# Output projection by seven products: weight sums by accumulating loads, a block's tail taken in steps, SyncE's loads in one chain

## The chip, the core and the metric

The kernel runs on one core of a Trainium2 chip. The core has a TensorE (PE, with its weight loads shown apart as PEld), a VectorE (DVE), a ScalarE (ACT), a GpSimd (POOL) and a SyncE (SP), and 16 DMA engines that all of its DMA queues share. SP and POOL issue the DMAs here. The metric is the device time of one launch in microseconds (us), and what counts is the median of the runs.

## The reference

One transformer block on 512 tokens of width 2048, in float32. The change touches one step of it, the output projection with the residual:

```python
x = x + g_a[:, None, :] * (jnp.concatenate([y_conv, y_attn], axis=-1) @ w_out[l])
h = modulate(rms_norm(x, norm_ffn[l]), sh_f, sc_f)
x = x + g_f[:, None, :] * ((jax.nn.silu(h @ ffn_w1[l]) * (h @ ffn_w3[l])) @ ffn_w2[l])
```

Here `w_out` is 2048 x 2048, `y_conv` and `y_attn` are 512 x 1024 each, and `g_a` is a row of gates made from the conditioning vector. What comes ahead of it (norm, `w_in`, a short convolution, sparse attention) and behind it (the feed-forward part) is unchanged.

## The kernel before, in words

**Seven products.** The projection is a product of two matrices cut into 2 x 2 blocks, and the kernel computes it with seven block products in place of eight, numbered 1 to 7. For each it needs a sum of blocks of `y` (a "form") and a sum of blocks of `w_out`. A block of `w_out` is 1024 x 1024 and is handled in eight pieces j = 0 to 7 of 128 x 1024 (512 KB). The pieces of a product's weights are `WB[p, j]`. Products 1, 5, 6 and 4 share one buffer for each j, the tile `wt`, because their weights grow out of one another: first W11 alone (product 1), then plus W12 (product 5), then plus W22 (product 6), then plus W21 (product 4). Product 2 has W21 alone, product 3 has W22 alone, product 7 has W12 plus W22. Signs are in the forms.

**Units.** The work is a list `yu` of 56 units (p, j), in this order: products 2, 1 and 5 with their eight pieces each (units 0 to 23); then 6 and 3 interleaved (24 to 39); then 7 (40 to 47) and 4 (48 to 55). A unit is twelve matmuls of 128 x 128 by 512 (line 1242): four output tiles, and three matmuls for each, because every operand is split into a high and a low part of reduced precision. Products 1, 6, 7 and 4 accumulate in the PSUM banks called "x" (tag `aux`), 5 and 3 in "y" and 2 in "z" (tag `main`).

**What a unit needs.** `y_load` (line 1182) fetches the weights, `y_split` (line 1216) makes the high part on ACT (line 1231) and the low part on DVE (line 1233), and `y_form` (line 1038) does the same for the form (lines 1043 and 1044). The high and low parts go into rings of three places, so a split can be about two units ahead of the matmuls. Only the split of (7,7) has places of its own (the tiles `w77`), and those of (4,5) to (4,7) too (`w4`).

**Loads.** The buffers of products 2 and 3 and of some pieces of 7 come from a ring of four places of 512 KB (the tiles `raw`); (3,4), (3,5), (7,4) and (7,5) lie in a part of the large tile `x2T`, and (7,0), (7,1) in tiles of the form H6 once that form has been used. Plain loads are issued by SP (queue q1). Loads that add to what lies in the buffer (`added`, line 1178, DMA with an add) are issued by POOL (queue q0). For product 5 the kernel before does both: for j < 4, SP loads W12 into a `raw` place called "b", and DVE adds it to `wt` (`w_sum`, line 1438); for j of 4 and more, POOL adds it by the DMA itself. The sum for product 6, `wt` plus `WB[3, j]`, is always one of DVE's (line 1446); it needs (3, j) and must stand behind the split of (5, j), since it overwrites the same buffer.

**The residual.** The blocks of x are loaded too: block (1,1) and (1,2) into `x2T` (line 1332), (2,2) into tiles of the form H3 (line 1335), (2,1) later. When a block of the product is complete, DVE multiplies it with the gates (`ga`, loaded by POOL) and adds it to x; ACT takes the sum of squares for the norm; POOL stores it. For block (1,1) that is `first_block` (lines 1372 to 1377), for the fifth product's share of (2,2) `fifth`, for the sixth's share of (1,2) `sixth`.

**The order.** The loop at line 1485 goes through units 6 to 55. In step n it first takes what `steps_at[n]` holds (loads and sums, set with `at_unit`), then splits unit n + 2, then writes the matmuls of unit n, then takes what `behind[n]` holds (forms, tails, stores, set with `behind_unit`). The program is then turned into one queue of instructions for each engine when it is built. That step may set an instruction ahead of others that are written before it, when it takes it to be ready sooner; `tc.issue_after(i)` forbids that: what it encloses stands behind `i` in that engine's queue, without waiting for `i` to finish. At run time each engine takes its queue strictly in order.

Of the kernel before, what the change touches and what calls it, by code (L numbers as in the profile page):

```python
# [70 lines left out]
def block_kernel(ctx: ExitStack, tc: tile.TileContext, a: dict, out: bass.AP):  # L71
    nc = tc.nc
    w_in, ada_w, w_out = a["w_in"][0], a["ada_w"][0], a["w_out"][0]
    w1, w3, w2 = a["ffn_w1"][0], a["ffn_w3"][0], a["ffn_w2"][0]
    x = a["x"][0]
# [301 lines left out]
    for name, n in ROWS.items():  # L377
        src = a[name].rearrange("l (k p) -> (l k) p", p=P) if name != "conv_w" else \
# [453 lines left out]
    class EarlyPlaces:  # L832
        n = 0
# [217 lines left out]
    ybank = {}  # L1051
    WB = {}
# [57 lines left out]
    class Places:  # L1110
        n = 0
# [45 lines left out]
    def y_units():  # L1157
        yield from ((p, j) for p in (2, 1, 5) for j in range(HK))
        for j in range(0, HK, 2):
            yield from ((6, j), (6, j + 1), (3, j), (3, j + 1)) if j in (0, HK - 2) else ((6, j), (3, j), (6, j + 1), (3, j + 1))  # L1160
        yield from ((p, j) for p in (7, 4) for j in range(HK))

    yu = list(y_units())
    yat = {u: n for n, u in enumerate(yu)}

    def w_block(r, c, j):
        k = (r - 1) * HK + j
        return w_out[k * P:(k + 1) * P, (2 - c) * 1024:(3 - c) * 1024].rearrange("p (a b) -> p a b", a=4)

    def in_four(t):  # L1170
        return t.rearrange("p (a b) -> p a b", a=4)

    def ring_place():
        return in_four(ring[0].tile([P, 1024], F32, tag="raw", name="raw"))

    added_last, loaded_last = [], [None]

    def added(to, src):
        with tc.issue_after(added_last[-1]) if added_last else ExitStack():
            added_last.append(nc.gpsimd.dma_start(to, src, accum_op=ALU.add).ins)  # L1180

    def y_load(p, j):
        if p == 2:
            WB[p, j] = ring_place()
            nc.sync.dma_start(WB[p, j], w_block(2, 1, j))
        elif p == 1:
            for q in (1, 5, 6, 4):
                WB[q, j] = in_four(WT[j])
            nc.sync.dma_start(WB[p, j], w_block(1, 1, j))
        elif p == 5 and j < 4:  # L1190
            WB["b", j] = ring_place()
            nc.sync.dma_start(WB["b", j], w_block(1, 2, j))
        elif p == 5:
            added(WB[p, j], w_block(1, 2, j))
        elif p == 3:
            WB[p, j] = x2T[:, 4 * j - 8:4 * j - 4, 0:HS] if j in (4, 5) else ring_place()
            nc.sync.dma_start(WB[p, j], w_block(2, 2, j))
        elif p == 7:
            if j < 2:
                to = WB[p, j] = YF["H6"][2 * j:2 * j + 2]  # L1200
            else:
                WB[p, j] = x2T[:, 4 * j - 8:4 * j - 4, 0:HS] if j in (4, 5) else ring_place()
                to = [WB[p, j]]
            for c in (1, 2):
                for n, t in enumerate(to):
                    src = w_block(c, 2, j)[:, 4 // len(to) * n:4 // len(to) * (n + 1)]
                    if c == 1:
                        loaded_last[-1] = nc.sync.dma_start(t, src).ins
                    else:
                        added(t, src)  # L1210
        elif p == 4:
            added(WB[p, j], w_block(2, 1, j))
# [54 lines left out]
    for n in range(-5, 6):  # L1267
        if n + 5 < HK:
            y_load(*yu[n + 5])
        if n + 2 >= 0:  # L1270
            y_split(*yu[n + 2])
        if n >= 0:
            y_multiply(*yu[n])
# [34 lines left out]
    twos = {}  # L1308

    def x2_of(r, c, t, n):  # L1310
        if (r, c) == (1, 1):
            return x2T[:, 4 * t + 2 * n:4 * t + 2 * n + 2, HS:S]
        if (r, c) == (1, 2):
            return x2T[:, HK + 4 * t + 2 * n:HK + 4 * t + 2 * n + 2, HS:S]
        if (r, c) == (2, 2):
            return YF["H3"][2 * t + n]
        return in_four(twos["x", t])[:, 2 * n:2 * n + 2]

    def x_of(r, c, t):
        i = 2 * (r - 1) + t  # L1320
        return x[i * P:(i + 1) * P, (2 - c) * 1024:(3 - c) * 1024]

    def x_load(r, c):
        for t in range(2):
            if r == 2:
                twos["x", t] = t2p.tile([P, 1024], F32, tag="t2", name="x21")
                to = in_four(twos["x", t])
            else:
                k0 = (c - 1) * HK + 4 * t
                to = x2T[:, k0:k0 + 4, HS:S]  # L1330
            with tc.issue_after(loaded_last[-1]) if r == 2 else ExitStack():
                nc.sync.dma_start(to, x_of(r, c, t).rearrange("p (a b) -> p a b", a=4))

    def x22_load(t, n):
        nc.sync.dma_start(x2_of(2, 2, t, n), x_of(2, 2, t)[:, n * 512:(n + 1) * 512].rearrange("p (a b) -> p a b", a=2))
# [1 line left out]
    def x_store(r, c, t):  # L1337
        i = 2 * (r - 1) + t
        for n in range(2):
            to = xd[n][:, t, :] if (r, c) == (2, 2) else \  # L1340
                out[0, i * P:(i + 1) * P, (2 - c) * 1024 + n * 512:(2 - c) * 1024 + (n + 1) * 512]
            nc.gpsimd.dma_start(to.rearrange("p (a b) -> p a b", a=2), x2_of(r, c, t, n))

    tags = ["d1", "d2"] * 64

    def two():
        return dp.tile([P, 512], F32, tag=tags[-1], name=tags.pop()).rearrange("p (a b) -> p a b", a=2)

    def pair_of(ps):
        return ps.rearrange("p (a b) -> p a b", a=2)  # L1350

    def gate_of(c, n):
        return pair_of(ga[:, (2 - c) * 1024 + n * 512:(2 - c) * 1024 + (n + 1) * 512])

    def squared(r, c, t, n, junk):
        nc.scalar.activation(junk, x2_of(r, c, t, n), AF.Square,
                             accum_out=ss2[:, 2 * (r - 1) + t, 2 * (2 - c) + n:2 * (2 - c) + n + 1])
# [8 lines left out]
    def copies(bank):  # L1366
        for t in range(2):
            twos[bank, t] = t2p.tile([P, 1024], F32, tag="t2", name=f"c{bank}")
            for n in range(2):
                nc.scalar.copy(twos[bank, t][:, n * 512:(n + 1) * 512], ybank[bank][2 * t + n])  # L1370

    def first_block(t, n):
        u, x2 = two(), x2_of(1, 1, t, n)
        nc.vector.tensor_add(u, pair_of(ybank["x"][2 * t + n]), pair_of(twos["z", t][:, n * 512:(n + 1) * 512]))
        nc.vector.tensor_mul(u, u, gate_of(1, n))
        nc.vector.tensor_add(x2, x2, u)
        squared(1, 1, t, n, u)
# [56 lines left out]
    def at_unit(p, j, *todo):  # L1434
        steps_at.setdefault(yat[p, j], []).extend(todo)

    def w_sum(to, j, one):
        nc.vector.tensor_add(WB[to, j], WB[to, j], WB[one, j])

    for j in range(HK):  # L1440
        at_unit(*yu[6 + j // 4 if j < 7 else 9], (y_load, 1, j))
        at_unit(*yu[6 + j if j < 4 else 7 + j], (y_load, 5, j))
        if j < 4:
            at_unit(*yu[12 + j], (w_sum, 5, j, "b"))
        at_unit(*yu[(13, 14, 15, 16, 17, 19, 25, 26)[j]], (y_load, 3, j))
        at_unit(*yu[yat[6, j] - 4], (lambda j: nc.vector.tensor_add(WB[6, j], WB[6, j], WB[3, j]), j))
        at_unit(*yu[(24, 25, 28, 30, 32, 34, 37, 38)[j]], (y_load, 7, j))
        at_unit(*yu[(27, 31, 35, 39, 40, 41, 42, 43)[j]], (y_load, 4, j))
    for q in (2, 3, 0, 1):
        at_unit(2, 7, (lambda q: nc.gpsimd.dma_start(ga[:, q * 512:(q + 1) * 512], gad[q].to_broadcast([P, 512])), q))  # L1450
    at_unit(1, 2, (x_load, 1, 1))
    at_unit(1, 4, (x_load, 1, 2))
    for q in range(4):
        at_unit(*yu[24 + 2 * q], (x22_load, q // 2, q % 2))
    at_unit(7, 3, (x_load, 2, 1))
    behind = {}

    def behind_unit(p, j, *todo):
        behind.setdefault(yat[p, j], []).extend(todo)
# [3 lines left out]
            behind_unit(*yu[n], (y_form, p, j))  # L1463
    behind_unit(2, 7, (copies, "z"))
    for q, (t, n) in enumerate(TN):
        behind_unit(5, (0, 1, 3, 4)[q], (first_block, t, n))
        behind_unit(*yu[(30, 32, 33, 35)[q]], (fifth, t, n))
        behind_unit(7, q, (gated, 1, 2, t, n, "y"))
    for t in range(2):
        behind_unit(6, 0, (x_store, 1, 1, t))  # L1470
        behind_unit(4, 2, (x_store, 1, 2, t))
        behind_unit(4, 1, (x_store, 2, 2, t))
    behind_unit(5, 7, (copies, "y"))
    behind_unit(6, 7, (sixth,))
# [10 lines left out]
    for n in range(6, len(yu)):  # L1485
# [4 lines left out]
        p, j = yu[n]  # L1490
# [573 lines left out]
    q, held = -1, []  # L2064
    for n, (b, p, j) in enumerate(units):
# [18 lines left out]
        if n + 5 < len(units):  # L2084
            w_sum(*units[n + 5])
# [40 lines left out]
```

## Time and profile before

| What | us |
|---|---|
| median of 3 runs (lowest, highest) | 2147.44 (2147.4, 2149.01) |
| the profiled execution, its own time | 2148.66 |
| its span, first to last instruction | 2146.9 |
| PE busy | 2117.9 (99%) |
| DVE busy | 1773.1 (83%) |
| first and last start of the projection's matmuls (line 1242) | 673.35 and 846.5 |
| PE idle inside that stretch, in two gaps | 0.68 and 8.33 |

The page gives each engine's busy time over the span. A row of a queue in order of time gives start, length, engine, line, operation, what it writes and reads, and in brackets how long the engine was idle before it and what ended that. A row of a stretch gives its length and then the busy time of PE, PEld, DVE, ACT and POOL, each with its number of instructions, then the clock that was granted to PE, the DMA engines' share and GB/s. In the DMA view a queue's row has packets, MB and its share of the 16 engines' time.

### The profile page before, as it was taken

How to read it: one execution, taken by the hardware profiler on the slowest of the kernel's cores; microseconds unless marked ns; L12 is line 12 of the kernel's file. 1: busy time of each engine (PE TensorE's matmuls, PEld its weight loads, DVE VectorE, ACT ScalarE, POOL GpSimd, SP SyncE). 2: the span in 40 equal slices, each digit the busy share in tenths (PEclk: the TensorE clock that was granted, in tenths of full speed). 3: DMA queues.
4: the chain of work that ended last, by engine and by line, in shares of the span. 5: the costliest groups of instructions: out<-in, count | busy, mean ns of one | idle time of the engine just before them, and what ended most of it. 6: DMA issues, size and time to landing. Idle time of an engine off the chain costs nothing.

```text
span 2146.9 us, 30986 instructions
## 1 busy us (share of the span) xinstructions
PE 2117.9 (99%) x11453; PEld 1778.9 (83%) x11453; DVE 1773.1 (83%) x2596; ACT 1043.2 (49%) x1665; POOL 254.9 (12%) x326
## 2 busy tenths in 40 slices
PE   7999999999999989999999999999999999999999
PEld 6778778888888868888888888888888887888887
DVE  7788658888788977888888888888888887878788
ACT  5226244555555547644444444444444555444543
POOL 0000200000000220001111111111111122211110
PEclk9999999999999999999999999999999999999999
DMA  9985638756668984598878877888787599797975
GB/s 339 363 272 192 201 100 252 217 163 206 179 184 272 258 199 138 139 248 206 201 191 189 209 196 187 203 195 203 184 202 182 144 301 295 145 307 138 290 157 139
DMA packets 452234, 450.20 MB, mean 210 GB/s; under 512 B 20707, under 2 KB 379147, under 8 KB 451442
## 3 DMA queue, kind: packets, MB, share of 16 engines
q1 hardware_dynamic: 379678, 333.00, 50.2%
q0 software_dynamic: 71872, 114.74, 26.9%
q8 instruction: 90, 1.47, 0.3%
q10 hardware_dynamic: 532, 0.48, 0.1%
q14 instruction: 62, 0.51, 0.1%
HBM read 428.19 MB, written 19.96 MB: 209 GB/s over the span
## 4 chain that ended last, share of the span: by engine, by line
PE 89%; DVE 4%; DMA 4%; issue 1%; SPq 1%; ACT 1%; ACTq 0%; DVEq 0%; POOLq 0%
PE main L1582 15%; PE aux L1582 11%; PE aux L1981 9%; PE main L1981 9%; PE main L1588 8%; PE aux L1588 6%; PE main L121 5%; PE main L123 5%; PE main L122 5%; PE aux L1242 2%; PE aux L121 2%; PE aux L989 2%; PE aux L123 2%; PE aux L122 2%; DMA raw<-in_w_out 1%
## 5 line engine op out<-in xcount | busy, mean ns | idle before, releaser
L1569 ACT CAST whi<-raw 128x1024 fp32r<-128x1024 f32 x246 | 257.6, 1051 | 259.1 <-PE main L1582 122.1
L1582 PE MATMUL main<-hC,whi 128*128 128x512 f32 x1408 | 347.1, 392 | 0.3 <-ACT whi L1569 0.2
L1576 DVE TENSOR_TENSOR wlo<-raw,whi 128x1024 fp32r<-128x1024 f32 x218 | 266.1, 1221 | 86.1 <-PE aux L1588 42.0
L1569 ACT CAST whi<-t 128x1024 fp32r<-128x1024 f32 x186 | 195.5, 1051 | 248.1 <-PE main L1981 62.1
L1582 PEld LDWEIGHTS main<-hC,whi 128*128 128x128 f32 x1408 | 256.9, 188 | 53.1 <-DVE d L1601 2.7
L1582 PE MATMUL aux<-hC,whi 128*128 128x512 f32 x1072 | 264.4, 391 | 0.0
L1582 PEld LDWEIGHTS aux<-hC,whi 128*128 128x128 f32 x1072 | 196.3, 188 | 38.2 <-issue 0.6
L1588 PEld LDWEIGHTS main<-hC,wlo 128*128 128x128 f32 x1408 | 184.9, 191 | 7.8
L1588 PE MATMUL main<-hC,wlo 128*128 128x256 f32 x1408 | 191.2, 283 | 0.0
L121 PE MATMUL main<-alo,whi 128*128 128x512 f32 x432 | 174.2, 404 | 0.0
L123 PE MATMUL main<-ahi,whi 128*128 128x512 f32 x432 | 170.3, 395 | 0.0
L122 PE MATMUL main<-ahi,wlo 128*128 128x512 f32 x432 | 169.1, 391 | 0.0
L1588 PE MATMUL aux<-hC,wlo 128*128 128x256 f32 x1072 | 148.5, 282 | 0.0
L1953 DVE TENSOR_TENSOR wlo<-t,whi 128x1024 fp32r<-128x1024 f32 x102 | 124.2, 1220 | 29.1 <-ACT whi L1569 29.0
L1588 PEld LDWEIGHTS aux<-hC,wlo 128*128 128x128 f32 x1072 | 142.1, 191 | 6.4
L1576 DVE TENSOR_TENSOR wlo<-t,whi 128x1024 fp32r<-128x1024 f32 x84 | 102.6, 1221 | 37.3 <-issue 13.4
L1981 PE MATMUL main<-wlo,ghi 128*128 128x512 f32 x304 | 118.5, 390 | 1.4 <-DVE wlo L1953 1.2
L1981 PE MATMUL aux<-whi,glo 128*128 128x512 f32 x308 | 119.8, 389 | 0.0
L1981 PE MATMUL aux<-whi,ghi 128*128 128x512 f32 x308 | 119.8, 389 | 0.0
L1981 PE MATMUL aux<-wlo,ghi 128*128 128x512 f32 x308 | 119.7, 389 | 0.0
L1981 PE MATMUL main<-whi,ghi 128*128 128x512 f32 x304 | 118.3, 389 | 0.0
L1981 PE MATMUL main<-whi,glo 128*128 128x512 f32 x304 | 118.3, 389 | 0.0
(426 smaller groups left out, 4173.7 us busy)
## 6 DMA issues: line engine op xcount, KB each, us to landing
raw<-in_ffn_w SPq DMA_DIRECT2D x204, 512.0 KB, 5.7
t<-in_ffn_w POOLq DMA_DIRECT2D x90, 512.0 KB, 6.8
t<-in_ffn_w SPq DMA_DIRECT2D x78, 512.0 KB, 5.9
araw<-in_ada_w SPq DMA_DIRECT2D x56, 512.0 KB, 8.7
raw<-in_w_in SPq DMA_DIRECT2D x128, 192.0 KB, 4.0
raw<-in_w_in SPq DMA_DIRECT2D x38, 512.0 KB, 4.9
kT<-in_ada_w SPq DMA_DIRECT2D x35, 512.0 KB, 4.4
accs<-in_ada_w POOLq DMA_DIRECT2D x64, 256.0 KB, 4.9
```

The source lines that it names most:

```text
L121: nc.tensor.matmul(ps, lhs[0], rhs[1], start=first, stop=False)
L122: nc.tensor.matmul(ps, lhs[1], rhs[0], start=False, stop=False)
L123: return nc.tensor.matmul(ps, lhs[0], rhs[0], start=False, stop=last).ins
L989: nc.tensor.matmul(po[:, b * HD:(b + 1) * HD], s["pT"][b][:, kb * P:(kb + 1) * P], vv[b][:, kb, g * HD:(g + 1) * HD], start=kb == 0, stop= ...
L1242: nc.tensor.matmul(ps, l, w, start=m == 0 and j == 0 and p in (1, 5, 2), stop=m == 2 and j == HK - 1 and p in (3, 2, 4), skip_group_check= ...
L1569: hi_ins[-1] = nc.scalar.copy(hi, t).ins
L1576: lo_ins[-1] = nc.vector.tensor_sub(lo, t, hi.bitcast(F32)).ins
L1582: nc.tensor.matmul(ps, wt[0][:, k * P:(k + 1) * P], hc(p, k), start=first and k == 0, stop=False, skip_group_check=True)
L1588: nc.tensor.matmul(ps[:, HS:], wt[1][:, k * P:(k + 1) * P], hc(p, k)[:, 0:HS], start=False, stop=last and k == HK - 1, skip_group_check=True)
L1953: W["last"] = nc.vector.tensor_sub(lo, t, hi.bitcast(F32)).ins
L1981: nc.tensor.matmul(ps[2 * t + c], x_[:, j, tok], w[:, cs], start=m == 0 and j == 0 and p in (1, 5, 2), stop=m == 2 and j == GS[b] - 1 and ...
```

## The change

There are five edits in the projection.

- The weight sums of product 5 are all made by accumulating loads on POOL: the four "b" loads of SP, their `raw` places and DVE's four sums are gone. The load for (5, j) stands at step 7 + j.
- A helper `chained` puts loads of SP into one chain, each behind the one before in SP's queue: x of blocks (1,1) and (1,2), (3,0) to (3,5) and the parts of (7,0) and (7,1) that SP loads. By the steps the chain runs x (1,1), x (1,2), (3,0) to (3,3), (7,0), (3,4), (7,1), (3,5). The loads of (3,4) and (3,5) go from steps 17 and 19 to 24 and 25, those of (3,0) to (3,3) from 13 to 16 to 15 to 18, x (1,1) one step forward.
- `first_block` is cut in two. `first_sum` (the add that empties the PSUM bank) stays behind the fifth product's units; the multiplication, the add to x and the squares go behind units 25, 27, 29 and 31. `fifth` goes from behind units 30, 32, 33, 35 to behind 33, 35, 38, 39.
- The stores of block (1,1) go from behind unit 24 to behind unit 33. Those of block (1,2) go from behind (4,2) to behind (7,1) and (7,3), and into the chain of POOL's accumulating loads.
- The accumulating loads (4,4) to (4,7) go from steps 40 to 43 to steps 42, 42, 44, 44.

```diff
-    added_last, loaded_last = [], [None]
+    added_last, loaded_last, chain = [], [None], []
+
+    def chained(to, src):
+        with tc.issue_after(chain[-1]) if chain else ExitStack():
+            chain.append(nc.sync.dma_start(to, src).ins)
+        return chain[-1]
...
-        elif p == 5 and j < 4:
-            WB["b", j] = ring_place()
-            nc.sync.dma_start(WB["b", j], w_block(1, 2, j))
         elif p == 5:
             added(WB[p, j], w_block(1, 2, j))
         elif p == 3:
             WB[p, j] = x2T[:, 4 * j - 8:4 * j - 4, 0:HS] if j in (4, 5) else ring_place()
-            nc.sync.dma_start(WB[p, j], w_block(2, 2, j))
+            (chained if j < 6 else nc.sync.dma_start)(WB[p, j], w_block(2, 2, j))
...
-                        loaded_last[-1] = nc.sync.dma_start(t, src).ins
+                        loaded_last[-1] = chained(t, src) if j < 2 else nc.sync.dma_start(t, src).ins
...
-            with tc.issue_after(loaded_last[-1]) if r == 2 else ExitStack():
-                nc.sync.dma_start(to, x_of(r, c, t).rearrange("p (a b) -> p a b", a=4))
+            src = x_of(r, c, t).rearrange("p (a b) -> p a b", a=4)
+            if r == 1:
+                chained(to, src)
+                continue
+            with tc.issue_after(loaded_last[-1]):
+                nc.sync.dma_start(to, src)
...
-            nc.gpsimd.dma_start(to.rearrange("p (a b) -> p a b", a=2), x2_of(r, c, t, n))
+            with tc.issue_after(added_last[-1]) if (r, c) == (1, 2) else ExitStack():
+                stored = nc.gpsimd.dma_start(to.rearrange("p (a b) -> p a b", a=2), x2_of(r, c, t, n)).ins
+            if (r, c) == (1, 2):
+                added_last.append(stored)
...
+    block1 = {}
+
+    def first_sum(t, n):
+        u = block1[t, n] = two()
+        nc.vector.tensor_add(u, pair_of(ybank["x"][2 * t + n]), pair_of(twos["z", t][:, n * 512:(n + 1) * 512]))
+
     def first_block(t, n):
-        u, x2 = two(), x2_of(1, 1, t, n)
-        nc.vector.tensor_add(u, pair_of(ybank["x"][2 * t + n]), pair_of(twos["z", t][:, n * 512:(n + 1) * 512]))
+        u, x2 = block1[t, n], x2_of(1, 1, t, n)
...
-        at_unit(*yu[6 + j if j < 4 else 7 + j], (y_load, 5, j))
-        if j < 4:
-            at_unit(*yu[12 + j], (w_sum, 5, j, "b"))
-        at_unit(*yu[(13, 14, 15, 16, 17, 19, 25, 26)[j]], (y_load, 3, j))
+        at_unit(*yu[7 + j], (y_load, 5, j))
+        at_unit(*yu[(15, 16, 17, 18, 24, 25, 25, 26)[j]], (y_load, 3, j))
...
-        at_unit(*yu[(27, 31, 35, 39, 40, 41, 42, 43)[j]], (y_load, 4, j))
+        at_unit(*yu[(27, 31, 35, 39, 42, 42, 44, 44)[j]], (y_load, 4, j))
...
-    at_unit(1, 2, (x_load, 1, 1))
+    at_unit(1, 1, (x_load, 1, 1))
...
-        behind_unit(5, (0, 1, 3, 4)[q], (first_block, t, n))
-        behind_unit(*yu[(30, 32, 33, 35)[q]], (fifth, t, n))
+        behind_unit(5, (0, 1, 3, 4)[q], (first_sum, t, n))
+        behind_unit(*yu[(25, 27, 29, 31)[q]], (first_block, t, n))
+        behind_unit(*yu[(33, 35, 38, 39)[q]], (fifth, t, n))
         behind_unit(7, q, (gated, 1, 2, t, n, "y"))
     for t in range(2):
-        behind_unit(6, 0, (x_store, 1, 1, t))
-        behind_unit(4, 2, (x_store, 1, 2, t))
+        behind_unit(*yu[33], (x_store, 1, 1, t))
+        behind_unit(7, (1, 3)[t], (x_store, 1, 2, t))
```

More of the change, by code (lines that the diff above doesn't have):

```diff
@@ L1435, in at_unit @@
         steps_at.setdefault(yat[p, j], []).extend(todo)
-    def w_sum(to, j, one):
-        nc.vector.tensor_add(WB[to, j], WB[to, j], WB[one, j])
     for j in range(HK):
         at_unit(*yu[6 + j // 4 if j < 7 else 9], (y_load, 1, j))
-        at_unit(*yu[6 + j if j < 4 else 7 + j], (y_load, 5, j))
-        if j < 4:
-            at_unit(*yu[12 + j], (w_sum, 5, j, "b"))
-        at_unit(*yu[(13, 14, 15, 16, 17, 19, 25, 26)[j]], (y_load, 3, j))
+        at_unit(*yu[7 + j], (y_load, 5, j))
+        at_unit(*yu[(15, 16, 17, 18, 24, 25, 25, 26)[j]], (y_load, 3, j))
         at_unit(*yu[yat[6, j] - 4], (lambda j: nc.vector.tensor_add(WB[6, j], WB[6, j], WB[3, j]), j))
         at_unit(*yu[(24, 25, 28, 30, 32, 34, 37, 38)[j]], (y_load, 7, j))
-        at_unit(*yu[(27, 31, 35, 39, 40, 41, 42, 43)[j]], (y_load, 4, j))
+        at_unit(*yu[(27, 31, 35, 39, 42, 42, 44, 44)[j]], (y_load, 4, j))
     for q in (2, 3, 0, 1):
         at_unit(2, 7, (lambda q: nc.gpsimd.dma_start(ga[:, q * 512:(q + 1) * 512], gad[q].to_broadcast([P, 512])), q))
-    at_unit(1, 2, (x_load, 1, 1))
+    at_unit(1, 1, (x_load, 1, 1))
     at_unit(1, 4, (x_load, 1, 2))
```

## The prediction, made before the result was known

> **What bounds the kernel now.** I read the page first, then the stretches of the output projection, then the queues of TensorE (PE), VectorE (DVE), ScalarE (ACT), SyncE (SP) and GpSimd (POOL) there in order of time, and last the DMA queues in short windows.
>
> ```profile
> span 2146.9 us, 30986 instructions
> PE 2117.9 (99%) x11453; PEld 1778.9 (83%) x11453; DVE 1773.1 (83%) x2596; ACT 1043.2 (49%) x1665; POOL 254.9 (12%) x326
> ```
>
> PE is idle for 29 us of 2146.9; every other engine can only cost time through those gaps. The change touches the projection alone (673 to 849 us), so what it can win is the idle time there, and what it can lose is a new gap.
>
> ```profile
> 753.80 0.50 PE L1242 MATMUL main<-wlo,form 128*128 128x512 f32 x1 [0.68 <-DVE wlo L1233]
> 753.80 3.06 PE main L1242 x12
> 756.85 2.72 PE aux L1242 x12
> 800.54 0.80 PE L1242 MATMUL aux<-wlo,form 128*128 128x512 f32 x1 [8.33 <-DVE wlo L1233]
> 801.13 1.05 PE L1242 MATMUL aux<-whi,form 128*128 128x512 f32 x2
> 804.56 0.61 PE L1242 MATMUL aux<-whi,form 128*128 128x512 f32 x2
> ```
>
> There are two gaps. A unit is 12 matmuls and takes 2.72 us (second chain row). After the first gap (0.68 us) a unit took 3.06, so that gap costs 0.68 + 0.34 = 1.0 us. After the second (8.33 us) the ten matmuls from 800.54 to 804.56 took 4.02 us where the pace is 10 x 2.72/12 = 2.27, so it costs 8.33 + 1.75 = 10.1 us. The doubled spacing is a clock matter: pairs take 1.05 and then 0.61 us. [...]
>
> What holds each gap? The second one first:
>
> ```profile
> 783.89 0.84 POOL L1180 DMA_DIRECT2D raw<-in_w_out  x1 [1.11 <-DVE wlo L1233]
> 797.15 1.14 ACT L1231 CAST w<-raw 128x512 fp32r<-128x512 f32 x2 [11.70 <-DMA raw<-in_w_out]
> 798.19 1.04 ACT L1231 CAST whi<-raw 128x1024 fp32r<-128x1024 f32 x1
> ```
>
> The two 512-wide casts are the split of (7,7), the only one in halves of a place of its own (w77). In ACT's queue it stands ahead of the split of (7,3), which PE needs four units earlier, and it waits for its accumulating load, issued at 783.89 and landed at 797.15. So an engine's queue does not follow the written order: it was laid down as if loads landed sooner than they do. DVE shows the same habit:
>
> ```profile
> 715.05 1.22 DVE L1233 TENSOR_TENSOR wlo<-wt,whi 128x1024 fp32r<-128x1024 f32 x1
> 716.52 1.22 DVE L1446 TENSOR_TENSOR wt<-wt,raw 128x1024 f32<-128x1024 f32 x1
> 717.66 1.21 DVE L1233 TENSOR_TENSOR wlo<-wt,whi 128x1024 fp32r<-128x1024 f32 x1
> 720.32 0.39 PE L1242 MATMUL main<-wlo,form 128*128 128x512 f32 x1
> ```
>
> Row 716.52 is the first L1446, the sum that adds the third product's weights (3,0) to place 0. It is written at step 20, beside the splits of units 21 and 22, yet it stands right behind the low part of (5,0) (715.05) and ahead of that of (5,1) (717.66), which PE uses at 720.32, at the start of unit 17. It did not wait, since (3,0) had landed. This place decides my forecast.
>
> **The change, part by part.** *Removed: four loads "b" and four sums.*
>
> ```profile
> L1192 SPq DMA_DIRECT2D raw<-in_w_out x4: 328/328/328, 682.5 to 690.2; - x4
> L1438 DVE TENSOR_TENSOR wt<-wt,raw x4: 1215/1216/1217, 698.3 to 706.1; 128x1024 f32<-128x1024 f32 x4
> ```
>
> 4 x 1.22 = 4.9 us of DVE go between 698 and 707. No PE gap lies there, and the low part of (5,1) was done at 718.87, 1.45 us ahead of its use: worth 0.
>
> *Added: four accumulating loads for (5,0) to (5,3).* Each can start when the low part of (1,j) is written, which for (1,0) is at 694.05 + 1.22 = 695.3, ten microseconds ahead of the first one now:
>
> ```profile
> 694.05 1.22 DVE L1233 TENSOR_TENSOR wlo<-wt,whi 128x1024 fp32r<-128x1024 f32 x1
> L1180 POOL DMA_DIRECT2D wt<-in_w_out x4: 840/858/895, 706.4 to 713.5; - x4
> DMA to landing us min/median/max: 8.3/10.1/11.3
> ```
>
> POOL's four issues (0.86 us each) hide, as it is 12% busy. For their own splits they land in time: (5,0) by 695.3 + 11.3 = 707, nine microseconds before its unit starts at 720.32 - 2.72 = 717.6, the others in turn. What matters is whom they meet. Windows 711:722 (accumulating loads running), 705:710 (almost none) and 701:706 (the gate loads `ga`) of the DMA view, then 694:700:
>
> ```profile
> q0 software_dynamic: 492, 1.82, 82.8%
> q1 hardware_dynamic: 488, 0.81, 22.8%
> ...
> q1 hardware_dynamic: 970, 1.72, 90.0%
> q0 software_dynamic: 47, 0.13, 11.0%
> ...
> q0 software_dynamic: 270, 0.88, 61.4%
> q1 hardware_dynamic: 487, 0.52, 32.2%
> ...
> q1 hardware_dynamic: 1158, 1.42, 74.5%
> q0 software_dynamic: 2, 0.01, 0.5%
> ```
>
> q0 is POOL's queue, q1 is SP's. Beside accumulating loads the two go packet for packet (492 to 488), and q1 gets 488/11 = 44 packets per us; alone it gets 970/5 = 194. The accumulating packets take nearly all the time, so whatever SP loads then crawls. [...]
>
> *Moved: SP's chain x, x, (3,0) to (3,3), (7,0), (3,4), (7,1), (3,5).*
>
> ```profile
> 694.21 0.93 SPq L1332 DMA_DIRECT2D x2T<-in_x  x2
> 696.29 0.99 SPq L1332 DMA_DIRECT2D x2T<-in_x  x2
> 699.51 5.54 SPq L1197 DMA_DIRECT2D raw<-in_w_out  x3
> ```
>
> SP's four loads of x write rows of 256 numbers, 1 KB packets: 4 x 512, and with (1,7) between them 128 more of 4 KB, 2176 in all. (3,0) is issued behind them, at about 697.3 instead of 699.5, since its ring place no longer waits for a "b". At 700, 1158 of the 2176 had gone (last pair of rows), and 1018 remain. Now the count: (5,0) with its 128 packets (512 KB at 4 KB) takes 128 of the 1018 along (2.9 us at 44 per us); `ga`, 256 packets, takes 256 x 487/270 = 460 (about 5 us); 430 are left at about 708. Before, q0 then rests until the accumulating load of 706.4 starts; now (5,1) to (5,7) follow without a pause (seven times about 3 us), so 430 packets of x at 44 per us last until 717.5, and the 128 packets of (3,0), 4 KB now and thus slower, until about 721.5. [...]
>
> With the sum (6,0) at its old place in DVE's queue, queued behind it are the low part of (5,1), the first sums and all later low parts. DVE waits until 724, sums (1.14), writes the low part (1.21), and PE starts unit 17 at 726.4 instead of 720.3: a new gap of 6.1 us, with a slow start of 1.75 (nearer to the gap of 8.33 than to that of 0.68). Bounds: 0 at a landing of 717.9, 11 + 1.75 at 729. (3,1) lands some 3 us later, by when DVE has work in hand: 0.
>
> *(3,4) and (3,5) behind (7,0), (7,1).*
>
> ```profile
> 735.59 1.01 SPq L1208 DMA_DIRECT2D H<-in_w_out  x1
> 744.12 1.21 DVE L1446 TENSOR_TENSOR wt<-wt,x2T 128x1024 f32<-128x1024 f32 x1
> ```
>
> The first row is the last load of (7,1), the second the sum that needs (3,5). If (3,5) follows that load at 736.6 and lands as slowly as the load of 743.55 further down (waited for until 751.38, 7.8 us), it is there at 744.4: 0, at most 3 if DVE, no longer behind, gets there sooner.
>
> *The first block in two parts, the fifth's later.* Eight operations (0.68 us, 0.60 apart, 4.8 us) leave DVE's full stretch for steps 25 to 31, and eight like them leave steps 30 to 35 for 33 to 39.
>
> ```profile
> 715.00:730.00 15.00, 15.00 (x68) 12.43 (x67) 15.00 (x21) 9.18 (x15) 0.56 (x1) 1.00 0.88 244
> 745.00:760.00 15.00, 14.32 (x63) 11.50 (x62) 13.10 (x19) 7.17 (x11) 0.84 (x1) 1.00 0.62 168
> 760.00:775.00 15.00, 15.00 (x68) 12.43 (x67) 11.56 (x16) 7.75 (x12) 3.02 (x3) 1.00 0.86 193
> 742.32 1.21 DVE L1233 TENSOR_TENSOR wlo<-raw,whi 128x1024 fp32r<-128x1024 f32 x1
> 743.55 0.33 SPq L1197 DMA_DIRECT2D raw<-in_w_out  x1
> 751.38 1.23 DVE L1446 TENSOR_TENSOR wt<-wt,raw 128x1024 f32<-128x1024 f32 x1 [1.90 <-DMA raw<-in_w_out]
> ```
>
> DVE (fifth column, after PE and PEld) has 1.9 and 3.4 us free in the later stretches, room for what comes net; without it up to 3 us would show. The relief also explains the only gain: the first gap hangs on (3,6), loaded at 743.55 when the low part of (3,0) is out of the ring place (743.53), and DVE waits for it at 751.38. A DVE that isn't behind writes that part about 1.2 us sooner, more than the 0.68: the gap goes, -1.0.
>
> *x's stores.* Those of block (1,1) (0.54 us each on POOL at their best) move to step 33, where POOL is 0.84 of 15 busy: 0. Those of (1,2) now stand between the accumulating loads (4,3) and (4,4) and wait for DVE's sums of that block, which sit behind the second gap (its end is 800.54). So (4,4) to (4,7), issued ahead of that gap now, are issued after it, some 15 us later. They stand behind (7,7) either way, so its landing is the same. They belong to the projection's last four units: with 10.1 us to land (the row of POOL's loads above) they come in time, taken as 0, at most 4 if a split of theirs stands early in ACT's queue.
>
> **Sum**, against the profiled execution (2148.66, a span of 2146.9 and 1.8 around it): 2148.66 + 6.1 + 1.75 - 1.0 = 2155.5. That execution lies 1.2 above the median of 2147.44, so the median comes to **2154.3 us**, slower by 0.3%.
>
> **Rivals.** *Loads in time.* If (3,0) lands by 717.9, or the sum stands later in DVE's queue, only the first gap goes: 2147.44 - 1.0 = 2146.4. For it: "b" is gone from SP's queue, and alone that queue moves 194 packets per us, by which the 1018 + 128 packets would take 5.9 us from 700 on and (3,0) would be there by about 708.5. Against it: the 44 packets per us. [...]
>
> *The second gap closes (faster).* If the split of (7,7) gets behind that of (7,3) in ACT's queue, or its load lands 9 us sooner, the 10.1 us go with the first gap's 1.0: 2136.3, or about 2144 with the new gap beside it. For it: queue orders are laid down anew with each edit. Against it: the loads that lead to (7,7) keep their steps, and the stores that now wait in the chain come behind it.
>
> *The store chain (slower).* The splits of (4,5) to (4,7) have places of their own as (7,7) has, and if they stand early in ACT's queue ACT waits for loads issued some 15 us later. Once ACT waits longer than the 2.72 us of a unit, PE stands: +2 to +4, 2150.5 without the new gap, 2158 with it.
>
> **How the numbers follow.** A change under 0.2% (4.3 us) can't be told from none. New gap at (6,0): 0.55, of which 0.41 come out over 4.3 us and 0.14 under. Loads in time: 0.20, no difference. Second gap closes: 0.18, faster. New gap and second gap closed: 0.03, no difference. Store chain alone: 0.04, half of it over 4.3. That makes faster 0.18, same 0.39, slower 0.43. The range leaves out the far end of the second gap's closing and the worst landing: 2139 to 2163; the forecast's own range is 2147 to 2163.
>
> **What would show it.** Right: a PE gap at about 720 released by DVE's wlo; an L1446 sum waiting for a w_out DMA just ahead of it; x2T loads taking over 20 us to land; the gap at 753 gone, that at 792 still there. Wrong: no wait at the first L1446 (the packet count failed), or a queue order in which that sum stands later, or (7,7)'s casts behind (7,3)'s.

## The result, and the profile after

The changed kernel takes **2159.49 us** (median of 4 runs, 2158.29 to 2163.08), the kernel before 2148.23 in the same comparison: ratio 1.0055, 95% interval 1.0038 to 1.0073, **11.3 us slower**. The forecast was 6.9 us slower (2154.3, range 2139 to 2163). The profiled execution took 2158.29.

The top of its page, then PE's longest waits over the whole kernel (sum, times, longest):

```profile
span 2156.5 us, 30990 instructions
PE 2119.5 (98%) x11453; PEld 1780.6 (83%) x11453; DVE 1768.7 (82%) x2592; ACT 1042.6 (48%) x1665; POOL 258.0 (12%) x330
```
```profile
PE aux L1245 <- DVE wlo L1236: 9.3, 1, 9.3
PE main L1245 <- DVE wlo L1236: 9.1, 1, 9.1
```

DVE does 4.4 us less (the four sums), and PE waits 9 us more. The 8.33 us wait of before is still there as the first row; the second is new. In the changed kernel `y_mm` is line 1245 (1242 before), the casts are 1234 (1231), the low parts 1236 (1233), the sums for product 6 1456 (1446), the accumulating loads 1186 (1180).

The new wait, in DVE's queue, ACT's and PE's in order of time, then the stretch 730:732 (its clock is the third number from the end):

```profile
713.65 1.23 DVE L1236 TENSOR_TENSOR wlo<-wt,whi 128x1024 fp32r<-128x1024 f32 x1 [1.16 <-ACT whi L1234]
714.79 0.42 DVE L1044 TENSOR_TENSOR form<-H,form 128x256 fp32r<-128x256 f32 x1
726.81 1.23 DVE L1456 TENSOR_TENSOR wt<-wt,raw 128x1024 f32<-128x1024 f32 x1 [11.60 <-DMA raw<-in_w_out]
727.96 0.68 DVE L1386 TENSOR_TENSOR d<-aux,cz 128x512 f32<-128x512 f32 x1
728.56 1.21 DVE L1236 TENSOR_TENSOR wlo<-wt,whi 128x1024 fp32r<-128x1024 f32 x1
```
```profile
715.28 1.05 ACT L1234 CAST whi<-wt 128x1024 fp32r<-128x1024 f32 x1 [1.36 <-PE aux L1245]
```
```profile
729.83 0.79 PE L1245 MATMUL main<-wlo,form 128*128 128x512 f32 x1 [9.14 <-DVE wlo L1236]
730.42 1.05 PE L1245 MATMUL main<-whi,form 128*128 128x512 f32 x2
733.70 0.39 PE L1245 MATMUL main<-wlo,form 128*128 128x512 f32 x1
```
```profile
730.00:732.00 2.00, 2.00 (x5) 1.61 (x6) 2.00 (x3) 0.00 (x0) 0.00 (x0) 0.50 1.03 335
```

The sum (6,0) stands where it stood before, right behind the split of (5,0), but now (3,0) is not there: DVE is idle for 11.60 us. Behind it in the queue stands a step of the first block (727.96) and then the low part that PE needs for unit 17, (5,1)'s (728.56). That low part had nothing to wait for: its cast on ACT (715.28) was done 10 us earlier. PE waits 9.14 us, and then starts slowly: the nine matmuls from 729.83 to 733.70 take 3.87 us where the pace of before is 9 x 2.72/12 = 2.04, and the granted clock was 0.50 in 730:732. DVE took its queue in order here: it spent the 11.60 us in front of work that was ready.

Why (3,0) was late: SP's queue, then the DMA view of 705:727.

```profile
696.50 8.35 SPq L1180 DMA_DIRECT2D raw<-in_w_out  x4
```
```profile
q0 software_dynamic: 1042, 3.73, 80.8%
q1 hardware_dynamic: 1047, 1.80, 24.7%
wt<-in_w_out POOLq DMA_DIRECT2D x4, 512.0 KB, 19.7
```

(3,0) is the first of the four, issued at 696.50 and in use at 726.81, 30 us later. For 22 us the two queues go packet for packet (1042 to 1047), and POOL's packets take 81% of the engines' time: 0.808 x 16 x 22 / 1042 = 273 ns each on average, against 83 ns for one of SP's by the same working. SP's queue gets 48 packets per us. The four accumulating loads issued in this stretch took a median of 19.7 us to land.

The second gap, in POOL's, ACT's and PE's queues:

```profile
794.18 0.84 POOL L1186 DMA_DIRECT2D raw<-in_w_out  x1 [0.95 <-DVE wlo L1236]
808.64 1.14 ACT L1234 CAST w<-raw 128x512 fp32r<-128x512 f32 x2 [12.69 <-DMA raw<-in_w_out]
809.69 1.04 ACT L1234 CAST whi<-raw 128x1024 fp32r<-128x1024 f32 x1
812.04 0.79 PE L1245 MATMUL aux<-wlo,form 128*128 128x512 f32 x1 [9.32 <-DVE wlo L1236]
```

The casts of (7,7) still stand ahead of (7,3)'s, and wait 12.69 us for a load issued at 794.18; 9.32 us of PE against 8.33. The first gap of before is gone: DVE still waits for (3,6), but briefly, and PE not at all (SP's queue, then DVE's):

```profile
754.12 0.33 SPq L1200 DMA_DIRECT2D raw<-in_w_out  x1
```
```profile
758.83 1.22 DVE L1456 TENSOR_TENSOR wt<-wt,raw 128x1024 f32<-128x1024 f32 x1 [1.12 <-DMA raw<-in_w_out]
```

So the projection loses 9.1 + 1.8 for the new gap and 1.0 more at the second, and wins 1.0: 10.9. The span grew by 9.6, since before waited once more in a late stage, which the changed kernel did not in this execution; PE's waits of before:

```profile
PE main L1981 <- DVE wlo L1953: 1.2, 1, 1.2
```

### The profile page after: what moved, and what is told of

It reads as the page before. It is cut to its first block, busy times and chain, and to the rows that moved or that the text cites. A ratio compares the mean times of both kernels' runs of the same rounds, so it can differ in the third digit from the quotient of the medians.

```text
span 2156.5 us, 30990 instructions
## 1 busy us (share of the span) xinstructions
PE 2119.5 (98%) x11453; PEld 1780.6 (83%) x11453; DVE 1768.7 (82%) x2592; ACT 1042.6 (48%) x1665; POOL 258.0 (12%) x330
## 4 chain that ended last, share of the span: by engine, by line
PE 91%; DMA 4%; DVE 2%; SPq 1%; issue 1%; ACT 1%; ACTq 0%; POOL 0%; DVEq 0%
PE main L1593 15%; PE aux L1593 11%; PE aux L1992 9%; PE main L1992 9%; PE main L1599 8%; PE aux L1599 6%; PE main L121 5%; PE main L123 5%; PE main L122 5%; PE aux L1245 3%; PE main L1245 3%; DMA raw<-in_w_out 2%; PE aux L121 2%; PE aux L123 2%; PE aux L122 2%; PE aux L989 2%
```

## The experiments

**Theory:** the time goes by places in queues. The four early accumulating loads slow down SP's queue, x and (3,0) land late, and that costs only because the sum (6,0) stands far ahead of where it is written. **Rivals:** the accumulating loads cost PE time by themselves; or SP's chain, with x ahead of (3,0), does.

**The weights ahead of x in the chain.**

```diff
-        at_unit(*yu[(15, 16, 17, 18, 24, 25, 25, 26)[j]], (y_load, 3, j))
+        at_unit(*yu[(7, 7, 8, 8, 24, 25, 25, 26)[j]], (y_load, 3, j))
```

> The changed kernel with (3,0) to (3,3) loaded at steps 7, 7, 8, 8, so that they stand ahead of the four x loads in SP's chain; every accumulating load stays. Theory (x and the weights share a queue that the accumulating loads slow down, and (3,0), the last in the chain, holds up DVE): (3,0) lands ahead of 710, the 9.1 us gap of PE at unit 17 and its slow start of 1.75 us are gone, 2148.6 us; x now lands near 727 to 731, and if DVE's additions of x (738 in the changed kernel, about 9 us earlier without the gap) wait for it, up to 3 us come back. Rival (the accumulating loads themselves hold up PE or DVE, whoever stands first in the chain): a gap of 6 us or more stays at unit 17, 2156 to 2160 us.

2149.75 us, against before 1.0006 (0.9997 to 1.0016). DVE's queue, then PE's:

```profile
715.07 1.22 DVE L1456 TENSOR_TENSOR wt<-wt,raw 128x1024 f32<-128x1024 f32 x1
...
749.42 1.23 DVE L1456 TENSOR_TENSOR wt<-wt,raw 128x1024 f32<-128x1024 f32 x1 [2.81 <-DMA raw<-in_w_out]
```
```profile
751.84 0.50 PE L1245 MATMUL aux<-wlo,form 128*128 128x512 f32 x1 [1.29 <-DVE wlo L1236]
```

The sum (6,0) has no wait, the gap at unit 17 is gone, the kernel is 9.7 us faster than the change, and x did not come too late. With DVE no longer behind, the old wait for (3,6) is back (2.81 us of DVE, 1.29 of PE).

**The sum at its written place.** Loads and their order as in the change.

```diff
+    def third_sum(j):
+        with tc.issue_after(low_of[-1]):
+            nc.vector.tensor_add(WB[6, j], WB[6, j], WB[3, j])
...
-        at_unit(*yu[yat[6, j] - 4], (lambda j: nc.vector.tensor_add(WB[6, j], WB[6, j], WB[3, j]), j))
+        at_unit(*yu[yat[6, j] - 4], (third_sum, j))
```

> The changed kernel with the sums of the sixth product's weights pinned in DVE's queue behind the low part of the split that is written just ahead of each; loads, their order and their landings stay as they are. Theory (the loss comes only from the place of the sum (6,0), far ahead of its written place): (3,0) still lands near 727, but the sum now stands seven splits further back, where DVE comes at about 727, so the gap at unit 17 shrinks to 1 us or less, 2148 to 2150 us. Rival (the slow landing of the accumulated weights (5,1) and on, or the crawl of the queues as such, holds PE): a gap of 6 us or more stays, 2156 to 2160 us.

2148.5 us, 0.9998 (0.9988 to 1.0007). DVE's queue around the sum (6,0), then the only PE gap between 690 and 850:

```profile
728.22 1.22 DVE L1236 TENSOR_TENSOR wlo<-wt,whi 128x1024 fp32r<-128x1024 f32 x1
729.36 1.22 DVE L1450 TENSOR_TENSOR wt<-wt,raw 128x1024 f32<-128x1024 f32 x1
```
```profile
801.06 0.79 PE L1245 MATMUL aux<-wlo,form 128*128 128x512 f32 x1 [8.89 <-DVE wlo L1236]
```

With every load as late as in the change, the sum comes at 729.36 without a wait, five low parts further back (seven were expected), and PE does not stop at unit 17. The edit pins all eight sums for product 6, but the only new gap hung on (6,0): its place is worth 2159.5 - 2148.5 = 11 us, all that the change lost.

**The "b" loads and DVE's sums put back**, the rest as changed.

```diff
+        elif p == 5 and j < 4:
+            WB["b", j] = ring_place()
+            nc.sync.dma_start(WB["b", j], w_block(1, 2, j))
...
-        at_unit(*yu[7 + j], (y_load, 5, j))
+        at_unit(*yu[6 + j if j < 4 else 7 + j], (y_load, 5, j))
+        if j < 4:
+            at_unit(*yu[12 + j], (lambda j: nc.vector.tensor_add(WB[5, j], WB[5, j], WB["b", j]), j))
```

> The changed kernel with the four plain loads b and the four DVE sums of the fifth product put back, so that the accumulating loads again begin with (5,4); SP's chain, the two-part first block and the moved stores stay. Theory (the four early accumulating loads slow down SP's queue): (3,0) lands ahead of 716 although it is last in the chain, the gap at unit 17 is gone, 2147 to 2149 us. Rival (the chain order x ahead of (3,0) delays it by itself, with or without those loads): (3,0) lands behind 720, a gap of 4 us or more stays, 2153 to 2160 us.

2147.84 us, 0.9998 (0.9989 to 1.0008). The sum (6,0) in DVE's queue:

```profile
716.25 1.21 DVE L1461 TENSOR_TENSOR wt<-wt,raw 128x1024 f32<-128x1024 f32 x1
```

No wait, with (3,0) behind x in the chain as in the change. So the chain's order alone does not delay it; the four early accumulating loads do, and only with x ahead of (3,0), as the run with the weights first showed. That rules out the second rival.

**The accumulating loads alone**, in the kernel before.

```diff
-        elif p == 5 and j < 4:
-            WB["b", j] = ring_place()
-            nc.sync.dma_start(WB["b", j], w_block(1, 2, j))
...
-        at_unit(*yu[6 + j if j < 4 else 7 + j], (y_load, 5, j))
-        if j < 4:
-            at_unit(*yu[12 + j], (w_sum, 5, j, "b"))
+        at_unit(*yu[7 + j], (y_load, 5, j))
```

> The kernel before with only the one edit that all eight sums of the fifth product's weights go by accumulating loads; no chain, no other step moved. SP's queue then has (3,0) to (3,3) ahead of x, at the place that the loads b had. Theory (those loads cost nothing by themselves, it takes a load that DVE waits for behind x): no gap at unit 17, 2146 to 2149 us. Rival (the four more accumulating loads cost by themselves, by late landings of (5,1) to (5,3) or by contention): a gap of 3 us or more between 715 and 735, 2151 us or more.

2153.59 us, 1.0022 (1.0013 to 1.0031): the rival's number, though not at its place. No gap between 715 and 735; most of the loss is at 755 (the gap at (7,3) is 0.8 us longer too, 9.17), in SP's, DVE's and PE's queues:

```profile
743.24 0.33 SPq L1194 DMA_DIRECT2D raw<-in_w_out  x1
```
```profile
752.77 1.23 DVE L1441 TENSOR_TENSOR wt<-wt,raw 128x1024 f32<-128x1024 f32 x1 [6.01 <-DMA raw<-in_w_out]
753.91 1.22 DVE L1230 TENSOR_TENSOR wlo<-wt,whi 128x1024 fp32r<-128x1024 f32 x1
```
```profile
755.18 0.79 PE L1239 MATMUL aux<-wlo,form 128*128 128x512 f32 x1 [4.06 <-DVE wlo L1230]
```

(3,6) is issued at the time of before (743.55 there) and lands 1.4 us later than there (752.77 to 751.38). But PE now waits at an `aux` unit, one of product 6, where before it waited at the `main` unit behind it: the sum (6,6) has moved ahead of one more low part. Is it the loads after all, or that place? Both edits together tell:

```diff
-        at_unit(*yu[yat[6, j] - 4], (lambda j: nc.vector.tensor_add(WB[6, j], WB[6, j], WB[3, j]), j))
+        at_unit(*yu[yat[6, j] - 4], (third_sum, j))
```

> The kernel before with all eight sums of the fifth product's weights by accumulating loads, as in the run of those loads alone, and besides that the sums of the sixth product's weights pinned in VectorE's queue behind the low part written just ahead of each. Theory (the 4.06 us at 755 in that run come from the place of the sum (6,6), one split further ahead in VectorE's queue than in the kernel before, and not from the loads): (3,6) still lands at about 751 to 753, but two more low parts stand ahead of its sum, the gap shrinks to 1.5 us or less, 2147 to 2150 us. Rival (the loads crowd (3,6) out, whatever the order): a gap of 3 us or more stays between 750 and 760, 2152 us or more.

2146.06 us, 0.9989 (0.9979 to 0.9999): no gap before the one at (7,3). The sums (6,5) and (6,6) in DVE's queue:

```profile
755.98 1.22 DVE L1432 TENSOR_TENSOR wt<-wt,x2T 128x1024 f32<-128x1024 f32 x1
761.25 1.22 DVE L1432 TENSOR_TENSOR wt<-wt,raw 128x1024 f32<-128x1024 f32 x1
```

The sum (6,6) now comes 8.5 us later than in the run before (752.77) and waits for nothing. With the sums at their written places, PE has no gap that the accumulating loads could have caused, and the first rival falls too. That the kernel is even a little faster than before shows elsewhere in the trace: the gap at (7,3) is 6.96 us where it was 8.33, for a reason that was not tested, and the one of 0.68 is gone.

**The second gap: (7,7)'s casts behind (7,6)'s**, in the kernel before; then in the change with the sums pinned, with the weights ahead of x, and with "b" put back.

```diff
-    low_of = [None]
+    low_of, high_of = [None], []
...
-        for h, l, s_ in todo:
-            nc.scalar.copy(h, s_)
+        with tc.issue_after(high_of[-1]) if (p, j) == (7, 7) else ExitStack():
+            for h, l, s_ in todo:
+                high_of.append(nc.scalar.copy(h, s_).ins)
```

> The kernel before with the casts of (7,7) pinned in ScalarE's queue behind those of (7,6), and nothing else. Theory (the second gap comes from the place of that split in ScalarE's queue, ahead of (7,3)'s): the gap of 8.33 us and its slow start of 1.75 us go, 10.1 us less than before, some 2138 to 2140 us, and no new gap of over 1 us behind it, since (7,7) lands at 797 and its unit would begin near 803. Rival (the accumulating loads of (7,4) to (7,7) and (4,j) are themselves too slow for PE at full pace): the gap moves to a later unit and 3 us or more of it stay, 2142 us or more.

> The changed kernel with both pins: the sums of the sixth product's weights behind the low part written just ahead of each, and the casts of (7,7) behind those of (7,6). Theory (two places in two queues are all that either kernel loses in the projection): no PE gap over 1 us between 690 and 850, 11 us less than before and 21 us less than the change, 2137 to 2140 us. Rival (the chain of the stores of (1,2) ahead of (4,4) to (4,7), whose ScalarE cast waited 2.5 us for its load with only the first pin, comes onto the path when PE runs on without the second gap): a new gap of 2 to 5 us at the units (4,3) to (4,5), 2141 to 2144 us.

> The changed kernel with (3,0) to (3,3) ahead of x in the chain and the casts of (7,7) pinned behind those of (7,6). Theory: the second gap (8.66 us with the first edit alone) goes with its slow start, the gap of 1.3 us at 752 stays, 2138 to 2141 us. Rival (the loads of (4,4) to (4,7) behind the stores come onto the path): a new gap of 2 to 5 us there, 2142 to 2145 us.

> The changed kernel with the four plain loads b and their DVE sums put back and the casts of (7,7) pinned behind those of (7,6). Theory (no part of the change but the early accumulating loads costs anything, and the first gap of the kernel before goes with the two-part first block): no PE gap over 1 us in the projection, level with the kernel that has both pins to 1.5 us, 2136 to 2140 us. Rival (putting the sums back on DVE costs it 4.9 us that PE feels once the gaps are gone): 3 us or more over the kernel with both pins.

| kernel | us | ratio to before (95%) | PE gap near 811 |
|---|---|---|---|
| before, (7,7) pinned | 2140.80 | 0.9961 (0.9946 to 0.9976) | 2.71 and 0.49 |
| change, both pins | 2143.55 | 0.9974 (0.9965 to 0.9983) | 3.71 |
| change, weights first, (7,7) pinned | 2144.97 | 0.9981 (0.9972 to 0.9991) | 3.57 |
| change, "b" back, (7,7) pinned | 2143.52 | 0.9970 (0.9959 to 0.9982) | 3.19 |

The gap at (7,3), which was 8.33, 8.89, 8.66 and 6.23 us in the traces without this pin, goes in all four, but only 4 to 8 us of the kernel's time go with it, and each kernel is 0.8 to 4 us slower than its theory allowed: a gap of 3 to 4 us comes back at (4,0). In the kernel before with the pin, ACT's queue, DVE's and PE's:

```profile
806.04 1.04 ACT L1232 CAST w<-wt 128x1024 fp32r<-128x1024 f32 x1 [6.18 <-DMA wt<-in_w_out]
806.99 1.04 ACT L1232 CAST whi<-wt 128x1024 fp32r<-128x1024 f32 x1
```
```profile
808.07 1.23 DVE L1234 TENSOR_TENSOR wlo<-wt,whi 128x1024 fp32r<-128x1024 f32 x1 [6.07 <-ACT whi L1232]
809.21 0.69 DVE L1363 TENSOR_TENSOR H<-H,d 128x512 f32<-128x512 f32 x1
809.81 1.28 DVE L1362 TENSOR_TENSOR d<-aux,ga 128x512 f32<-128x512 f32 x2
```
```profile
810.55 0.50 PE L1243 MATMUL aux<-wlo,form 128*128 128x512 f32 x1 [2.71 <-DVE d L1362]
```

The first cast writes a tile `w` of 1024, so it is the first split of product 4 with a place of its own, (4,5). It waits 6.18 us for its load, with the next cast in turn behind it; DVE's low part of that one (808.07) stands ahead of the steps (L1362) that empty the bank which (4,0) needs. The gap is also there in the kernel before, which has no stores in POOL's chain: the rival named for the change with both pins met its number (2143.55) mostly by another cause. The stores can have added a little: with both pins the same cast waits longer.

```profile
806.91 1.05 ACT L1235 CAST w<-wt 128x1024 fp32r<-128x1024 f32 x1 [7.68 <-DMA wt<-in_w_out]
```

**All four splits with places of their own pinned:** the condition of the last diff becomes

```diff
-        with tc.issue_after(high_of[-1]) if (p, j) == (7, 7) else ExitStack():
+        with tc.issue_after(high_of[-1]) if (p, j) == (7, 7) or p == 4 and j > 4 else ExitStack():
```

> The kernel before with the casts of all four splits that have places of their own, (7,7), (4,5), (4,6) and (4,7), pinned in ScalarE's queue behind those of the split written ahead of each. Theory (the 3.2 us that came back at 808 to 813 when (7,7) alone was pinned are the same habit a third time: the cast of (4,5) stands ahead of (4,1)'s, waits 6.2 us for its load, and VectorE's step that frees the bank for (4,0) is queued behind (4,1)'s low part): no PE gap over 1 us between 755 and 840, 3 us less than with (7,7) alone, 12 to 13 us less than before, 2136 to 2138 us. Rival (by then the loads of (4,3) to (4,7), which land every 2.75 us up to 812, are themselves the pace): a gap of 2 us or more stays at a later unit, 2140 us or more.

> The changed kernel with the sums of the sixth product's weights pinned and the same four casts pinned. Theory: the gap of 3.7 us at 811 and its slow start go, 5 us less than with (7,7) alone, 2137 to 2140 us, level to 2 us with the kernel before under the same four pins, so that the change itself is worth nothing once the queues are in order. Rival (the stores of (1,2) in the chain hold back (4,5) to (4,7), which landed at 804 to 814 with (7,7) alone): a gap of 2 us or more at (4,5) to (4,7), 3 us or more behind the other.

The kernel before with these four pins: **2137.21 us, 0.9947 (0.9933 to 0.9960)**. The change with them and the pinned sums: **2137.53 us, 0.9949 (0.9936 to 0.9961)**. The stretches 690:760 and 760:850, first of the change, then of the change with the pins (length, then PE's busy time first; the clock is third from the end):

```profile
690.00:760.00 70.00, 60.86 (x261) 49.90 (x260) 53.63 (x77) 37.28 (x65) 16.30 (x21) 0.93 0.91 237
760.00:850.00 90.00, 80.68 (x389) 67.50 (x389) 64.20 (x96) 51.67 (x96) 17.63 (x21) 0.94 0.75 179
```
```profile
690.00:760.00 70.00, 70.00 (x311) 57.97 (x310) 64.34 (x93) 43.18 (x74) 17.28 (x22) 1.00 0.93 258
760.00:850.00 90.00, 90.00 (x467) 76.86 (x466) 68.98 (x111) 60.23 (x124) 18.81 (x24) 1.00 0.75 188
```

In the change with the pins, PE has no gap left in the projection and the full clock throughout. The loads (4,3) to (4,7) were not the pace. The change is worth nothing measurable beside the kernel before (0.3 us between the medians, intervals that cover each other). The two do not have quite the same pins: the sums of the kernel before are not pinned, and it keeps its first gap:

```profile
754.49 0.50 PE L1243 MATMUL main<-wlo,form 128*128 128x512 f32 x1 [0.97 <-DVE wlo L1234]
```

The kernel before with its sums pinned as well was not run; by this row it could be about 1 us faster (an estimate).

## Why the prediction was right in kind, and where it fell short

- *The bound:* right. The second gap of before hung on the place of (7,7)'s casts: pinned, it went, without touching a load. The new gap hung on the place of (6,0) in the same way. For the first gap of before (0.68) it is not shown alone; it was gone where the sums were pinned along with the four more accumulating loads.
- *Four sums less on DVE, worth 0:* right. Put back, they cost nothing (2147.84), even with (7,7) pinned (2143.52 against 2143.55).
- *DVE waits until 724 for (3,0):* the mechanism was right, the size 2.8 us short (726.81). The step that failed is the packet count of x. The DMA view's totals for 693:700, 700:710 and 710:722:

```profile
DMA packets 1150, 1.43 MB, mean 205 GB/s; under 512 B 32, under 2 KB 1056, under 8 KB 1150
DMA packets 1213, 2.74 MB, mean 274 GB/s; under 512 B 112, under 2 KB 691, under 8 KB 1212
DMA packets 1108, 2.86 MB, mean 238 GB/s; under 512 B 83, under 2 KB 525, under 8 KB 1106
```

  x's packets are those between 512 B and 2 KB: 1024, then 579, then 442, of 2048. So 445 were left at 710, where the count had 430 at 708 (2 us late already); and they went at 442/12 = 37 per us, not 44, because the 44 had counted every packet of q1. In 710:722 q1 moved 552, of which 110 were not x's (tiny ones and the first of the loads behind x):

```profile
q1 hardware_dynamic: 552, 0.81, 21.6%
```

  x was done at about 722, not 717.5 (+4.5); (3,0) then took 4.8 us, not 4 + 2.5 (-1.7). Together +2.8: two errors that in part cancelled, which is luck. No run shows the 2.5 us that the forecast's 724 has on top of the count's 721.5; in the changed kernel the 4.8 are all that (3,0) took behind x. Larger packets went slower, as the count had it: in 722:727 SP's had 3.6 KB on average against 1.5 in 710:722, and took 0.366 x 16 x 5 / 191 = 153 ns each against 75, with 38 per us against 46.

```profile
q1 hardware_dynamic: 191, 0.69, 36.6%
```

- *A new gap of 6.1 us:* it was 9.14. Of the 3.0 us, 2.8 are the landing and 0.6 the step of the first block (727.96 to 728.56) that stood between the sum and the low part and was not in the forecast; 0.4 come off, as PE stopped at 729.83 - 9.14 = 720.7 and not at 720.3. The slow start was 3.87 - 2.04 = 1.8, as forecast (1.75); the granted clock was 0.50 in 730:732, as it was in 800.5:803 of the kernel before, where pairs took 1.05 us, against 1.00 in 804.5:806.5 there, where a pair took 0.61.
- *The first gap goes, -1.0:* it went, but hardly for the reason given (a DVE that is less behind): (3,6) was there 4.7 us after its issue (754.12 to 758.83) where it took 7.8 before. So this term came out by luck as far as the runs show. With the sums pinned the gap stayed away; with the weights first, 1.29 us came back. What the two-part block has in this was not separated.
- *The second gap unchanged:* it grew by 1.0, with (7,7)'s load 14.4 us on its way in place of 13.2.
- *The stores of (1,2) in POOL's chain, 0, at most 4:* 0 as far as seen; with all pins the change is level with the kernel before.
- *"The store chain" as a rival* named the early casts of (4,5) to (4,7). They exist, in both kernels, but cost PE time only once the second gap is gone.
- *Loads in time, second gap closes:* neither happened. The accumulating loads took a median of 19.7 us (705:727), several of them queued beside SP's traffic.
- *A slip without weight:* (5,0) was said to land nine microseconds before its unit; by the numbers beside it (707 and 717.6) it is 10.6.

The sum's terms come to +3.0 at the new gap and +1.0 at the second, 4.0 of the 4.4 us between forecast and result.

## What to carry to other kernels

Look for the instruction that waits at the head of an in-order queue while work that could run stands behind it: here three such places cost the changed kernel 22 us (2159.5 to 2137.5), and order constraints, which move an instruction in its own queue and add no wait for another engine, gave them back. Before a load is made later or slower, find who waits for it and where that one stands in its engine's queue. When a gap is closed, read the queues again, for the next early instruction shows itself only then.

## What the runs showed of the hardware

A DMA that adds was not the cheap replacement of a plain load and a sum here: beside it, SP's queue moved 48 packets per us (705:727 of the changed kernel) where it moved 194 in the kernel before with POOL's queue almost empty (705:710, 47 packets of POOL's). Both queues advanced packet for packet (1042 to 1047), and a packet of POOL's queue took about 273 ns on average, worked out from its share of the engines' time. With four such loads more, of 512 KB each, (3,0) was on the way for 30.3 us (696.50 to 726.81), and x for about 28 (693.39 to about 722, an estimate from the packet counts). Yet with the sums pinned this cost nothing: 2148.5 us for the change and 2146.06 for the kernel before with the four loads, with no PE gap in the projection ahead of the one at (7,3) in either.
